# Eight feed-forward tile pairs done jointly instead of six, fewer dense matmuls between attention's steps, and two groups of vector work with a higher priority

## The chip, the cores and the metric

The kernel runs on one core of one Trainium2 chip. The metric is the device time of one execution in microseconds; lower is better. Of three timed runs the median is 1756.36 us (1756.19 to 1757.58).

## The reference

One layer of a hybrid decoder, 1024 tokens wide and long (D = S = 1024), in float32:

```
u = rmsnorm(x);  proj = u @ w_in
y_a = rwkv7_mix(token_shift(p_rwkv), ...)          # 8 heads of 64
y_b = dsa_attention(q, k, v, q_idx, k_idx, w_idx)  # 8 heads of 64, causal, top 256 keys by an indexer
merged = sigmoid(g_a) * (y_a @ w_o_rwkv) + sigmoid(g_b) * (y_b @ w_o_att)
h = x + merged @ w_out
z_gate, z_up = split(rmsnorm(h) @ w_ffn_in)        # 1024 -> 2 x 2816
h = h + (silu(z_gate) * z_up) @ w_ffn_out          # 2816 -> 1024
return rmsnorm(h)
```

## The kernel before

The tokens are cut in two halves of HT = 512. Activations lie transposed, 8 planes of 128 channels by 512 tokens. Every large matrix product is done in three matmuls for each 128-row plane of the contraction: high part of the weights by high part of the activations (L143), high by low (L144), low by high (L148). `split` makes such a pair: ACT copies x to `hi` (L117), DVE subtracts it to give `lo` (L118). Weights come by DMA on SP's queue into `wst` (ring of 3) and are split into `whi` and `wlo` (rings of 2). Results gather in PSUM: 3 banks `acc`, 5 banks `mix`.

The feed-forward part has 22 tiles of 128 columns (gate and up each) in three groups: `GROUPS = [(0, 8), (8, 8), (16, 6)]`. For the first two groups each half does `ffn_in` (the two products, then silu times up) and `ffn_out` (a partial product with `w_ffn_out`, 128 output channels at a time, added to the residual that lies in DRAM as `d_h`: load, add at L1388, store). The third group (`JOINT = 2`) is done for both halves at once by `joint`: as in Winograd's form of Strassen's scheme, the four block products of a tile pair become 7 products of 12 matmuls each, 84 where two halves apart take 96. For it DVE and ACT make sums and differences of the activations of both halves: T1 (from L1604), T2 (L1592, L1610) and the split of B22 ahead of the joint loop, T3 (L1592) and T4 (L1633, L1634) inside its first round. `h` is normalised there by L1575 with `row` (L287 spreads it on PE, L294 copies it). The old activations of half 0 are read back from `d_z`. m1 and m2 are the products with half 0's own planes `za` and `zb`; m1 and m2 of the first two pairs stand ahead of the loop, those of pair j + 2 in round j: T1, m1, T2, B22, T3, m2, T4. The result of each round goes to DRAM (`d_f`), and `reload` brings it back as an `ffn_out` operand, `fhi`/`flo` for half 0 and `fj` for half 1.

What sets the order. PE's order is the order of the program text (`manual_schedule`). A queue `fill` holds generators of dense matmuls, and `pump(n)` issues about n of them between the steps of something else. The attention of half 1 (`attend`, 4 head pairs of 4 query blocks, 16 units) yields after each step how many to pump: logits (L1100, then on DVE bias and minimum L1102, on ACT the exponential L1105), transposes (L1114, copied by ACT at L1116), values (L1124). While it runs, the fill is ffn_in and ffn_out of half 0. The order of the other engines is made by a list scheduler; `tc.high_priority()` moves what stands under it ahead. Each engine does its own list in that order, and waits where an operand isn't there.

At the end: attention of half 1, `merge` (w_o, w_out, the residual h of half 1), then `joint`, in whose front the rest of the fill, ffn_out of half 0, group 1, is issued (`run(*fill)`) between L287 and m1; then dense tiles of half 1 with ffn_out and norm of half 0 between them, ffn_out of half 1, and `finish_out`: the last group's partial product for half 1, the last residual add and the norm, transposed for the last 128 tokens.

In `normalise` (half 0, in the first group, while RWKV runs) `zb`, planes 4 to 7 of the normalised activations, is split last.

Of the kernel before, what the change touches and what calls it, by code (L numbers as in the profile page):

```python
# [12 lines left out]
F32R = mybir.dt.float32r  # L13
# [6 lines left out]
ALU = mybir.AluOpType  # L20
# [3 lines left out]
S = 1024  # L24
HT = 512
NFF = 22
GROUPS = [(0, 8), (8, 8), (16, 6)]
JOINT = 2
TOPK = 256
C1 = math.exp(-0.5)  # L30
# [20 lines left out]
def block_kernel(ctx: ExitStack, tc: tile.TileContext, ins: dict, outT: bass.AP, outR: bass.AP, stop=None, dbg=None):  # L51
# [64 lines left out]
    def split(hi, lo, x):  # L116
        A.activation(hi, x, AF.Copy)  # L117
        V.tensor_tensor(lo, x, hi.bitcast(F32), op=ALU.subtract)  # L118
# [8 lines left out]
    def weights(src, nk=8, rush=True, st=None, pool=None):  # L127
        with tc.high_priority() if rush else nullcontext():
            if st is None:
                st = raw_weights(src, nk)  # L130
            hi, lo = ((pool or wp).tile([128, nk, 128], F32R, tag=tag, name=tag, bufs=8 if pool else None)
                      for tag in ("whi", "wlo"))
            split(hi, lo, st)
        return hi, lo
# [115 lines left out]
    def opened(side, name, **kw):  # L250
        stack = ExitStack()
        return stack, stack.enter_context(tc.tile_pool(name=name, bufs=1, side=side, reuse_waits="tile", **kw))
# [810 lines left out]
    def attend(half, p, bias):  # L1063
# [112 lines left out]
        for i in range(len(units) + 2):  # L1176
            if i < len(units):
                hp, bi = units[i]
                if i == 0:
                    kqv[hp] = load(hp)  # L1180
                    load_q(hp, 0)
                    load_q(hp, 1)
                if bi == 2 and hp < 3:
                    kqv[hp + 1] = load(hp + 1, sms[hp][:, 0, :] if half else None)
                    load_q(hp + 1, 0)
                    load_q(hp + 1, 1)
                if bi == 0:
                    sms[hp] = smp.tile([128, 4, 2], F32, tag="sm", name="sm", bufs=3)
                Ls[i] = []
            for e in range(2):  # L1190
                if i < len(units):
                    Ls[i].append(logits(hp, bi, e, kqv[hp], sms[hp]))
                    yield 4 if half else (bi + 3) // 2
                if 0 <= i - 1 < len(units):
                    ptss.setdefault(i - 1, []).append(turn(units[i - 1][1], Ls[i - 1][e]))
                    yield 3 if half else (units[i - 1][1] + 3) // 2
            if i >= 2:
                hp2, bi2 = units[i - 2]
                if bi2 == 0:
                    pys[hp2] = mix()  # L1200
                values(bi2, ptss.pop(i - 2), kqv[hp2], pys[hp2])
                if bi2 == 3:
                    ri = close1(sms[hp2])
                yield 3 if half else bi2 + 1
                if bi2 == 3:
                    closing.append((2, hp2, ri))
                elif closing:
                    close(closing)
# [85 lines left out]
    def normalise(zp, sq, row):  # L1294

        h = sq.h

        def one(k, out):
            V.scalar_tensor_tensor(out, h[:, k, :], par[:, P_N2 + k:P_N2 + k + 1], row, op0=ALU.mult, op1=ALU.mult)
            SY.dma_start(d_z[k], out)  # L1300

        low, ts = zp.tile([128, 8, HT], F32R, tag="s2", name="za"), []
        for k in range(4):
            one(k, h[:, k, :])
            split(low[:, k, :], low[:, 4 + k, :], h[:, k, :])
        for k in range(4):
            ts.append(tmp() if k < 3 else tp.tile([128, HT], F32, tag="sacc", name="zt", bufs=2))
            one(4 + k, ts[k])
        high = zp.tile([128, 8, HT], F32R, tag="s0", name="zb")
        for k in range(4):  # L1310
            split(high[:, k, :], high[:, 4 + k, :], ts[k])
        return [Planes(*(a + b)) for a, b in zip(parts(low), parts(high))]

    def ffn_in(zp, tags, zs, gi, box):
# [47 lines left out]
    def ffn_out(half, zp, f, gi, sqs=None):  # L1362
        gn = GROUPS[gi][1]
        final = sqs is not None
        if final:
            h = zp.tile([128, 8, HT], F32, tag="s2", name="h")
            sqs.append(Rms(h))
            for d in range(8):
                G.dma_start(h[:, d, :], d_h[half][d])

        def w(d):
            return weights(ins["w_fo1"][d] if final else ins["w_fo0"][gi, d], gn)

        bank = mix if final else acc
        pss = [bank() for _ in range(1 if final else 2)]
        last = yield from but_last(mm3_last(pss, [w(d) for d in range(len(pss))], f, gn, within=half == 1))
        for d in range(8):
            if final:
                t = h[:, d, :]
            else:  # L1380
                t = tmp()
                SY.dma_start(t, d_h[half][d])
            if d < len(pss):
                ps = pss[d]
            else:
                ps = bank()
                last = yield from but_last(mm3(ps, w(d), f, nk=gn))
            V.tensor_tensor(t, t, ps, op=ALU.add)  # L1388
            if final:
                sqs[0].add(d)  # L1390
            else:
                SY.dma_start(d_h[half][d], t)
            if d >= len(pss) - 1:
                yield last
# [25 lines left out]
    def finish_out(half, zp, f):  # L1420

        gn, n = GROUPS[-1][1], HT - 128
        tok, last = slice(0, n), slice(n, HT)
        h = zp.tile([128, 8, HT], F32, tag="s1", name="h")
        for d in range(8):
# [63 lines left out]
            V.tensor_scalar(out[:, 512:768], hT[:, 512:768], rs, None, op0=ALU.mult)  # L1491
            SY.dma_start(outR[:, 512:1024], out[:, 512:1024])

    def ffn(half, zp, zs, tags):

        for gi in range(JOINT):
            f = []
            yield from ffn_in(zp, tags, zs, gi, f)
            yield from ffn_out(half, zp, f[0], gi)

    def joint(z0, zp0, zs1, zp1, md, after):

# [262 lines left out]
    sz0, zp0 = zps[0]  # L1765
    sr.close()
    with tc.tile_pool(name="at1", bufs=1, side="right", reuse_waits="tile") as ap:
        pump(130)
        for n in attend(1, ap, bias):
            pump(abs(n))  # L1770
    sb.close()
    (sz1, zp1), zs1, sq0 = opened("right", "zp1"), [], []
    smd, md = opened("right", "md")
    stage_j = joint(z0[0], zp0, zs1, zp1, md,
                    lambda z1: fill.append(ffn(1, zp1, [z1, None], ("s3", "s0"))))
    run_over(merge(1, zp1, zs1, next(stage_j)))
    next(stage_j)
    smd.close()
    fj = act_tiles(zp0, "f", ("s1", "s0"))
    reload(0, fj)  # L1780
    credit[0] = 0
    pump_whole(144 - 8)
    run_over(ffn_out(0, zp0, fj, JOINT, sq0))
    pump_whole(48)
    run_over(norm_out(0, sq0[0]))
    pump(300)
    sz0.close()
    sfj, fp = opened("right", "fj")
    fj = tuple(fp.tile([128, GROUPS[JOINT][1], HT], F32R, name=f"fj{i}") for i in range(2))
    reload(1, fj)  # L1790
    run(*fill)
    finish_out(1, zp1, fj)
    sfj.close()
    sz1.close()


# [20 lines left out]
def _layout(x, norm1_g, w_in, tshift_mu, w_decay_up, w0, a_up, a0, g_up, k_k, k_a, r_k,  # L1817
# [8 lines left out]
    a = {}  # L1826
# [26 lines left out]
    wi = cols(w_ffn_in)  # L1853
    a["w_ffn_in"] = np.ascontiguousarray(np.stack([wi[:NFF], wi[NFF:]], axis=1).reshape(2 * NFF, 128, 8, 128))
    wo = cols(w_ffn_out)
    a["w_fo0"] = np.ascontiguousarray(np.stack([wo[:, :, 0:8], wo[:, :, 8:16]], axis=0))
    a["w_fo1"] = np.ascontiguousarray(wo[:, :, 16:22])
    return a


# [15 lines left out]
```

## Time and the profile before

| | |
|---|---|
| median of 3 runs | 1756.36 us |
| the profiled execution | 1753.59 us, span 1751.7 us |
| mean granted clock of TensorE | 0.988 |
| PE busy | 97% |
| DVE, ACT, POOL busy | 64%, 50%, 8% |
| DMA | 253 MB, 145 GB/s over the span |

The page's times are those of one execution. A group's line names the source line, the engine, the operation, out<-in, the shape and the count, then the busy time and what ended the idle time before it. PE's busy time is modelled and overlaps between neighbouring matmuls, so the cost of a matmul is read from the distance between starts, not from its own length.

### The profile page before, as it was taken

What the parts mean: (1) busy time and instruction counts of PE and PEld (TensorE: products, weight loads), DVE (VectorE), ACT (ScalarE), POOL (GpSimd) and SP (SyncE); (2) the same over time, 40 slices, a digit from 0 to 9 for tenths busy, and PEclk for the clock granted to TensorE, in tenths of its full rate; (3) what the DMA queues carried; (4) which work ended last, traced back from release to release, by engine and by line L of the source; (5) the groups of instructions that cost most, each with busy time, mean ns of one, the idle gap of its engine ahead of it and who ended that gap; (6) DMA issues with size and microseconds to landing.
All of it is one profiled execution on the core that took longest, in us unless ns stands there. A gap on an engine that the chain in (4) does not pass through costs nothing.

```text
span 1751.7 us, 26667 instructions
## 1 busy us (share of the span) xinstructions
PE 1694.3 (97%) x10000; PEld 1395.7 (80%) x10000; DVE 1127.6 (64%) x2206; ACT 869.6 (50%) x1685; POOL 133.8 (8%) x183
## 2 busy tenths in 40 slices
PE   8999999999999999999999999999979999999997
PEld 6888888888878777877787888888857788888887
DVE  6789899866577567858856544466577655433344
ACT  6365998554455788665334365533334333222322
POOL 0000000010022110001000311011000100000001
PEclk9999999999999999999999999999989999999999
DMA  5542334545376436734343764266622633553362
GB/s 209 178 139 87 107 91 141 174 108 160 109 214 169 146 102 197 225 112 137 90 121 100 228 172 127 91 226 203 187 83 90 193 112 108 172 168 102 115 214 80
DMA packets 144448, 253.44 MB, mean 145 GB/s; under 512 B 49680, under 2 KB 71888, under 8 KB 144192
## 3 DMA queue, kind: packets, MB, share of 16 engines
q1 hardware_dynamic: 115760, 161.84, 29.8%
q10 hardware_dynamic: 16128, 48.60, 8.8%
q0 software_dynamic: 12432, 41.30, 8.1%
q8 instruction: 79, 1.29, 0.3%
q14 instruction: 49, 0.40, 0.1%
HBM read 193.45 MB, written 58.25 MB: 144 GB/s over the span
## 4 chain that ended last, share of the span: by engine, by line
PE 41%; issue 6%; DVE 2%; DMA 1%; ACT 1%; POOL 1%; POOLq 0%; DVEq 0%; ACTq 0%
PE acc L148 9%; PE acc L143 9%; PE acc L144 9%; PE acc L161 3%; PE mix L1124 1%; PE mix L1100 1%; PE mix L1114 1%; PE mix L1548 1%; PE mix L1546 1%; PE mix L1545 1%; PE mix L148 1%; PE mix L144 1%; PE mix L143 1%; DMA wst<-in_w_ffn_in 0%; DMA d_h<-tmp 0%
## 5 line engine op out<-in xcount | busy, mean ns | idle before, releaser
L118 DVE TENSOR_TENSOR wlo<-wst,whi 128x1024 fp32r<-128x1024 f32 (+1 forms) x203 | 248.1, 1223 | 246.0 <-ACT whi L117 130.0
L117 ACT ACTIVATE whi<-wst 128x1024 fp32r<-128x1024 f32 (+1 forms) x203 | 212.6, 1049 | 278.4 <-PE acc L144 212.5
L143 PE MATMUL acc<-u1hi,whi 128*128 128x512 f32 x320 | 127.9, 400 | 0.0
L144 PE MATMUL acc<-u1lo,whi 128*128 128x512 f32 x320 | 125.1, 391 | 0.0
L143 PE MATMUL acc<-u0hi,whi 128*128 128x512 f32 (+1 forms) x320 | 122.8, 386 | 0.0
L144 PE MATMUL acc<-u0lo,whi 128*128 128x512 f32 (+1 forms) x320 | 121.3, 382 | 0.0
L143 PE MATMUL acc<-s,whi 128*128 128x512 f32 x256 | 99.8, 390 | 0.0
L144 PE MATMUL acc<-s,whi 128*128 128x512 f32 x256 | 99.6, 389 | 0.0
L143 PE MATMUL acc<-fhi,whi 128*128 128x512 f32 x192 | 76.9, 401 | 12.6 <-DVE tmp L1388 12.6
L148 PE MATMUL acc<-u1hi,wlo 128*128 128x512 f32 x320 | 81.8, 394 | 0.0
L148 PE MATMUL acc<-u0hi,wlo 128*128 128x512 f32 (+1 forms) x320 | 78.6, 384 | 0.0
L144 PE MATMUL acc<-flo,whi 128*128 128x512 f32 x192 | 76.0, 396 | 0.0
L1015 ACT ACTIVATE junkl<-kept,z 128x1024 int8<-128x1024 int16 (+1 forms) x64 | 69.4, 1084 | 4.7 <-DVE kept L984 4.4
L143 PEld LDWEIGHTS acc<-u1hi,whi 128*128 128x128 f32 x320 | 60.1, 188 | 12.6 <-issue 0.9
L1105 ACT ACTIVATE L<-L,mx 128x128 f32<-128x128 f32 (+7 forms) x64 | 49.5, 774 | 41.4 <-DVE mx L1102 40.8
L143 PEld LDWEIGHTS acc<-u0hi,whi 128*128 128x128 f32 x320 | 60.2, 188 | 11.9 <-issue 0.4
L144 PEld LDWEIGHTS acc<-u1lo,whi 128*128 128x128 f32 x320 | 60.2, 188 | 11.3
L144 PEld LDWEIGHTS acc<-u0lo,whi 128*128 128x128 f32 x320 | 60.2, 188 | 11.0
L148 PEld LDWEIGHTS acc<-u1hi,wlo 128*128 128x128 f32 x320 | 58.9, 188 | 12.5 <-issue 0.9
L148 PEld LDWEIGHTS acc<-u0hi,wlo 128*128 128x128 f32 x320 | 58.1, 188 | 11.9 <-issue 0.7
L148 PE MATMUL acc<-s,wlo 128*128 128x512 f32 x256 | 63.2, 389 | 0.0
L148 PEld LDWEIGHTS acc<-s,wlo 128*128 128x128 f32 x256 | 48.0, 188 | 10.0
(476 smaller groups left out, 4080.7 us busy)
## 6 DMA issues: line engine op xcount, KB each, us to landing
wst<-in_w_ffn_in SPq DMA_DIRECT2D x61, 512.0 KB
wst<-in_w_in ACTq DMA_DIRECT2D x36, 512.0 KB
wst<-in_w_in SPq DMA_DIRECT2D x27, 512.0 KB
wst<-in_w_fo SPq DMA_DIRECT2D x25, 512.0 KB
k<-d_k POOLq DMA_DIRECT2D x24, 512.0 KB, 8.0
d_g<-tmp ACTq DMA_DIRECT2D x32, 256.0 KB
wst<-in_w_ffn_in ACTq DMA_DIRECT2D x16, 512.0 KB
tmp<-d_h SPq DMA_DIRECT2D x32, 256.0 KB
```

The lines of the kernel that those rows point to most:

```text
L117: A.activation(hi, x, AF.Copy)
L118: V.tensor_tensor(lo, x, hi.bitcast(F32), op=ALU.subtract)
L143: T.matmul(ps, whi[:, wk + k, :], ahi[:, ak + k, tok], start=k == 0, stop=False)
L144: T.matmul(ps, whi[:, wk + k, :], alo[:, ak + k, tok], start=False, stop=False)
L148: T.matmul(ps, wlo[:, wk + k, :], ahi[:, ak + k, tok], start=False, stop=k == nk - 1)
L161: T.matmul(ps, w[:, k, :], a[:, k, tok], start=k == 0 and j == 0, stop=k == nk - 1 and j == 2)
L1015: A.activation(junka[:, :n], y, AF.Sign, bias=z[:, i:i + 1], accum_out=cnt[:, i:i + 1])
L1100: T.matmul(ps[:, :w], q[bi // 2][:, e, bi % 2 * 128:bi % 2 * 128 + 128], k[:, i, e, c:c + w], start=i == 0, stop=i == 1)
L1105: A.activation(L[:, :n], L[:, :n], AF.Exp, scale=-1.0, bias=last, accum_out=sm[:, bi, e:e + 1])
L1114: T.transpose(ps[:, j * 128:(j + 1) * 128], L[:, (c + j) * 128:(c + j + 1) * 128], ident)
L1124: T.matmul(py[64 * e:64 * e + 64, bi * 128:(bi + 1) * 128], v[:, j, 64 * e:64 * e + 64], pts[e][j // 4][:, j % 4, :], start=j == b, stop=j ...
L1545: T.matmul(ps, whi[:, k, :], hi[k], start=opens and k == 0, stop=False, skip_group_check=True)
```

## The change

- `GROUPS` becomes `[(0, 8), (8, 6), (14, 8)]`: 8 pairs are done jointly, and the second group has 6 tiles. The host's layout of `w_ffn_out` follows (`w_fo0` holds the two groups of 8, `w_fo1` that of 6).
- In half 1, attention pumps 3, 2 and 2 after logits, transposes and values, where it pumped 4, 3 and 3; ahead of it `pump(100)` instead of `pump(130)`.
- In `normalise` the splits of zb have high priority (the late split).
- In `ffn_out`, where it isn't the final one, the residual add has high priority.
- For half 1 the joint group is reloaded right after half 0's, and its ffn_out comes after the first dense group; the group of 6 stays in SBUF and is what `finish_out` multiplies last.

```diff
-GROUPS = [(0, 8), (8, 8), (16, 6)]
+GROUPS = [(0, 8), (8, 6), (14, 8)]
...
-                    yield 4 if half else (bi + 3) // 2
+                    yield 3 if half else (bi + 3) // 2
...
-                    yield 3 if half else (units[i - 1][1] + 3) // 2
+                    yield 2 if half else (units[i - 1][1] + 3) // 2
...
-                yield 3 if half else bi2 + 1
+                yield 2 if half else bi2 + 1
...
-        for k in range(4):
-            split(high[:, k, :], high[:, 4 + k, :], ts[k])
+        with tc.high_priority():
+            for k in range(4):
+                split(high[:, k, :], high[:, 4 + k, :], ts[k])
...
-            return weights(ins["w_fo1"][d] if final else ins["w_fo0"][gi, d], gn)
+            return weights(ins["w_fo1"][d] if gi == 1 else ins["w_fo0"][gi // 2, d], gn)
...
-            V.tensor_tensor(t, t, ps, op=ALU.add)
+            with nullcontext() if final else tc.high_priority():
+                V.tensor_tensor(t, t, ps, op=ALU.add)
...
-        gn, n = GROUPS[-1][1], HT - 128
+        gn, n = GROUPS[1][1], HT - 128
...
-    def ffn(half, zp, zs, tags):
+    def ffn(half, zp, zs, tags, fj=None, kept=None):
...
-            yield from ffn_out(half, zp, f[0], gi)
+            if gi == 0 or kept is None:
+                yield from ffn_out(half, zp, f[0], gi)
+            else:
+                kept.append(f[0])
+            if gi == 0 and fj is not None:
+                yield from ffn_out(half, zp, fj, JOINT)
...
-        pump(130)
+        pump(100)
...
+    fj1, f1 = [], []
     stage_j = joint(z0[0], zp0, zs1, zp1, md,
-                    lambda z1: fill.append(ffn(1, zp1, [z1, None], ("s3", "s0"))))
+                    lambda z1: fill.append(ffn(1, zp1, [z1, None], ("s3", "s0"), fj1, f1)))
...
     reload(0, fj)
+    sfj, fp = opened("right", "fj")
+    fj1.extend(fp.tile([128, GROUPS[JOINT][1], HT], F32R, name=f"fj{i}") for i in range(2))
+    reload(1, fj1)
...
-    pump(300)
+    run(*fill)
+    fill.clear()
+    sfj.close()
     sz0.close()
-    sfj, fp = opened("right", "fj")
-    fj = tuple(fp.tile([128, GROUPS[JOINT][1], HT], F32R, name=f"fj{i}") for i in range(2))
-    reload(1, fj)
-    run(*fill)
-    finish_out(1, zp1, fj)
-    sfj.close()
+    finish_out(1, zp1, f1[0])
```

The lines above L1388 keep their numbers or move by one; those below move by 2 to 8 (the residual add L1388 is L1390 after, L1575 is L1582, L1604 is L1611, L1592 is L1599, L1610 is L1617, L1645 is L1652, L1554 is L1561).

How the order moves, at three places. First PE in attention, at the fourth block of a head pair (512 wide logits), before:

```order
L1124 MATMUL mix<-pt,v 64x128 x10
L1100 MATMUL mix<-k,q 128x512 x4
L143 MATMUL acc<-zb,whi 128x512
L144 MATMUL acc<-zb,whi 128x512
L143 MATMUL acc<-zb,whi 128x512
L144 MATMUL acc<-zb,whi 128x512
L1114 MATMUL mix<-kc,L 128x128 x7
L148 MATMUL acc<-za,wlo 128x512 x4
L1100 MATMUL mix<-k,q 128x512 x4
L148 MATMUL acc<-zb,wlo 128x512 x4
L1114 MATMUL mix<-kc,L 128x128 x7
L1124 MATMUL mix<-pt,v 64x128 x12
```

and with the change:

```order
L148 MATMUL acc<-za,wlo 128x512 x4
L1124 MATMUL mix<-pt,v 64x128 x10
L1100 MATMUL mix<-k,q 128x512 x4
L148 MATMUL acc<-zb,wlo 128x512 x4
L1114 MATMUL mix<-kc,L 128x128 x7
L1100 MATMUL mix<-k,q 128x512 x4
L1114 MATMUL mix<-kc,L 128x128 x7
L143 MATMUL acc<-za,whi 128x512
L144 MATMUL acc<-za,whi 128x512
L143 MATMUL acc<-za,whi 128x512
L144 MATMUL acc<-za,whi 128x512
L1124 MATMUL mix<-pt,v 64x128 x12
```

The dense matmuls (L143, L144, L148) between the first transposes and the second logits, and between those and the second transposes, are gone. Over the whole attention of half 1 the dense matmuls between steps go from 272 to 195, and the pairs of steps with none between them from 16 to 35.

Second, DVE in the joint front. Before, from the last of T2's and B22's splits (the `s` tiles here) on, with the residual adds L1388 behind:

```order
L118 TENSOR_TENSOR s_12329<-h,s_12329 128x512
L1592 TENSOR_TENSOR t_12324<-h 128x512
L118 TENSOR_TENSOR s_12296<-t_12314,s_12296 128x512
L1610 TENSOR_TENSOR t_12322<-t_12322,t_12324 128x512
L118 TENSOR_TENSOR s_12329<-h,s_12329 128x512
L1388 TENSOR_TENSOR tmp<-tmp,acc 128x512
L118 TENSOR_TENSOR s_12296<-t_12322,s_12296 128x512
L1388 TENSOR_TENSOR tmp<-tmp,acc 128x512 x2
```

and with the change, from the start of the normalisation on (here `s` is T1):

```order
L1582 SCALAR_TENSOR_TENSOR h<-h,par,row 128x512 x2
L1611 TENSOR_TENSOR t_12119<-h,t_12119 128x512
L1611 TENSOR_TENSOR t_12125<-h,t_12125 128x512
L1582 SCALAR_TENSOR_TENSOR h<-h,par,row 128x512
L1390 TENSOR_TENSOR tmp<-tmp,acc 128x512
L118 TENSOR_TENSOR wlo<-wst,whi 128x768
L118 TENSOR_TENSOR s_12117<-t_12119,s_12117 128x512
L118 TENSOR_TENSOR s_12117<-t_12125,s_12117 128x512
L1611 TENSOR_TENSOR t_12131<-h,t_12131 128x512
L1582 SCALAR_TENSOR_TENSOR h<-h,par,row 128x512
L1390 TENSOR_TENSOR tmp<-tmp,acc 128x512
```

The residual adds stand among T1's operations now, each ahead of the splits of T1 that follow it; one more comes behind the last rows shown. ffn_out of half 0 has 56 matmuls left behind L287 where it had 88.

Third, ACT at the second joint pair, before (`whi` is for m1 of the fourth pair, `sw` are sums of weights):

```order
L117 ACTIVATE sw<-sr 128x512
L117 ACTIVATE sw<-wst 128x512
L1665 ACTIVATE tmp<-u_12630 128x512
L117 ACTIVATE s_12571<-tmp 128x512
L117 ACTIVATE whi<-wst 128x1024
```

and with the change (L1652 copies the round's first product, m5):

```order
L117 ACTIVATE sw<-sr 128x512
L117 ACTIVATE sw<-wst 128x512
L1652 ACTIVATE tmp<-acc 128x512
L117 ACTIVATE whi<-wst 128x1024
L117 ACTIVATE sw<-sr 128x512
L1561 ACTIVATE tmp<-mix 128x512
```

Here the copy stands ahead of `whi`; at the zb splits, which the priority of `normalise` is about, ACT's and DVE's rows are the same before and after.

More of the change, by code (lines that the diff above doesn't have):

```diff
@@ L1855, in _layout @@
     wo = cols(w_ffn_out)
-    a["w_fo0"] = np.ascontiguousarray(np.stack([wo[:, :, 0:8], wo[:, :, 8:16]], axis=0))
-    a["w_fo1"] = np.ascontiguousarray(wo[:, :, 16:22])
+    a["w_fo0"] = np.ascontiguousarray(np.stack([wo[:, :, 0:8], wo[:, :, 14:22]], axis=0))
+    a["w_fo1"] = np.ascontiguousarray(wo[:, :, 8:14])
     return a
```

## The prediction

> **What bounds the kernel now.** I read the engine totals first, then the list of what PE waits for, then the three places in that list which the change touches, in the timeline.
>
> ```profile
> span 1751.7 us, 26667 instructions
> PE 1694.3 (97%) x10000; PEld 1395.7 (80%) x10000; DVE 1127.6 (64%) x2206; ACT 869.6 (50%) x1685; POOL 133.8 (8%) x183
> ```
>
> PE is busy 97% of the span, so the kernel ends when PE has gone through its list. A change pays in two ways only: fewer matmuls, or fewer waits between them. The price of one matmul comes from two stretches without a wait (columns: stretch, length, busy time and count of PE, PEld, DVE, ACT, POOL, granted clock, DMA share, GB/s); three stretches used below stand with the first.
>
> ```profile
> 1550.00:1600.00 50.00, 50.00 (x222) 41.42 (x221) 17.79 (x20) 12.01 (x13) 0.00 (x0) 1.00 0.49 142
> ...
> 998.90:1137.00 138.10, 137.44 (x1022) 114.95 (x1022) 66.21 (x164) 80.24 (x157) 19.82 (x37) 1.00 0.46 126
> 1256.50:1283.40 26.90, 14.33 (x63) 11.61 (x62) 23.99 (x37) 9.88 (x15) 2.79 (x5) 0.85 0.45 145
> 1283.40:1321.10 37.70, 35.93 (x151) 28.78 (x150) 26.15 (x42) 14.33 (x23) 2.19 (x4) 0.97 0.21 70
> ```
>
> 50 us hold 222 matmuls of 128x512: 0.225 us each, at full clock. The waits of PE, longest first (us in total, times, longest):
>
> ```profile
> PE acc L143 <- DVE tmp L1388: 12.6, 1, 12.6
> PE acc L427 <- ACT u0hi L300: 6.9, 1, 6.9
> PE mix L622 <- DVE x L698: 3.4, 1, 3.4
> PE acc L143 <- ACT zb L117: 3.3, 1, 3.3
> ...
> PE mix L1545 <- DVE tmp L1670: 1.7, 1, 1.7
> ...
> PE mix L1545 <- ACT s L117: 1.2, 1, 1.2
> ...
> PE mix L1546 <- DVE s L118: 0.6, 2, 0.3
> PE mix L1100 <- ACT pt L1116: 0.5, 2, 0.3
> ```
>
> The longest one stands in front of the joint tiles. PE needs a free bank of `acc`, which the residual add of L1388 frees, and that add stands on DVE behind the splits of T1, T2 and B22. The timeline of PE and DVE there (start, length, engine, line; in brackets the idle time before and its releaser):
>
> ```profile
> 1254.81 1.05 PE L287 MATMUL mix<-kc,rs 128*128 128x128 f32 x8
> 1282.97 0.77 PE L143 MATMUL acc<-fhi,whi 128*128 128x512 f32 x1 [12.57 <-DVE tmp L1388]
> 1283.54 0.63 PE L144 MATMUL acc<-flo,whi 128*128 128x512 f32 x1
> 1285.67 0.44 PE L143 MATMUL acc<-fhi,whi 128*128 128x512 f32 x1
> 1321.46 0.86 PE L1548 MATMUL mix<-s,sw 128*128 128x512 f32 x3
> ...
> 1256.53 1.41 DVE L1575 SCALAR_TENSOR_TENSOR h<-h,par,row 128x512 f32<-128x512 f32 x2 [1.47 <-ACT row L294]
> 1281.55 0.68 DVE L118 TENSOR_TENSOR s<-h,s 128x512 fp32r<-128x512 f32 x1
> 1282.15 0.68 DVE L1388 TENSOR_TENSOR tmp<-tmp,acc 128x512 f32<-128x512 f32 x1
> 1282.75 0.68 DVE L118 TENSOR_TENSOR s<-t,s 128x512 fp32r<-128x512 f32 x1
> 1259.72 1.22 DVE L118 TENSOR_TENSOR wlo<-wst,whi 128x1024 fp32r<-128x1024 f32 x1
> 1260.86 1.28 DVE L118 TENSOR_TENSOR s<-t,s 128x512 fp32r<-128x512 f32 x2
> 1266.36 0.69 DVE L1604 TENSOR_TENSOR t<-h,t 128x512 f32<-128x512 f32 x1 [1.69 <-DMA t<-d_z]
> 1278.53 0.69 DVE L1610 TENSOR_TENSOR t<-t,t 128x512 f32<-128x512 f32 x1 [1.20 <-DMA t<-d_z]
> ```
>
> DVE works through 23.99 us in 26.90 while PE stands; successive 128x512 operations start 0.60 us apart (1281.55, 1282.15, 1282.75) and a 1024-wide split takes 1.14 (1259.72 to 1260.86). After the wait the matmuls run at half clock: from 1283.54 to 1285.67 five of them start 0.43 us apart. That costs some 1.4 us more with the slow first one (0.57).
>
> **The sum, part by part.** Time zero for the joint front is the start of L287 (1254.81); the matmul count between any two points is from the order of both kernels.
>
> *Eight pairs, not six.* A joint pair has 7 products of 12 matmuls, 84, where two separate tiles have 96. Two pairs more are 24 matmuls less, and the order of PE holds just that: 24 x 0.225 = **-5.4 us**. The additional transforms of weights fall on DVE, ACT and SP, in the joint loop; its cover there is PE's own 84 matmuls (18.9 us) per pair against some 11 us of DVE work, worked out as about 18 operations of 0.60. If the cover failed, each pair would wait on L1670 or the weight splits, as the 1.7 us did once before.
>
> *Residual adds in front.* Before, T4's last matmuls start at 1321.46 and end 0.7 later, at t = 67.3. Between L287 and the joint products PE has 88 matmuls of ffn_out before and 56 now, 32 less (7.2 us, which moved elsewhere and are no gain), so like for like the old front ends at 60.1. Now DVE starts on the normalisation at t = 1.7. It has the same splits, but each add of a finished ffn_out tile stands between T1's operations and frees its bank as PE ends the tile (every 18 x 0.225 = 4.1 us); the 12.6 us wait has no cause left. In exchange DVE's T1 splits queue behind those adds, each waiting for PE. From there to T2's last split the new order has 35 operations of 128x512 (three of them adds), a 768-wide and two 1024-wide weight splits: 35 x 0.60 + 0.86 + 2 x 1.14 = 24.1 us, so t = 25.8 if nothing waits; with the two waits for d_z of before, 1.69 and 1.20, it is 28.7, and I take 29. Unhindered, PE would reach T2 after 0.8 us of L287 and 128 matmuls, at 29.6, and T4's end after 188, at 43.1; so DVE is late next, at T4 above all. From T2's last split to T4's last split the order has 32 operations of 0.60 and a split of 1.14, 20.3 us; T4 then ends one us later (its four last matmuls), at 29 + 20.3 + 1.0 = 50.3. Gain: 60.1 - 50.3 = 9.8. Against it I set 1.3 us at the second pair, whose `whi` split now stands on ACT behind the copy of m5 (bounds 0 and the 2.7 us of one product of 12), and 0.5 for the clock. Together **-8.0 us**. Bounds: the same way took 37.70 us before, in step with PE, which was busy 35.93 of them; DVE's own part was 26.15 (row 1283.40, 42 operations). If the new one needs all 26.15, the gain is 60.1 - 56.2 = 3.9; if nothing waits, 60.1 - 43.1 = 17.0. I take the count of operations, since residual adds and weight splits that swelled the old row stand earlier now.
>
> The clock, by rows: a wait of 1.75 us was followed by matmuls at full clock, one of 3.34 by half clock.
>
> ```profile
> 821.93 0.80 PE L143 MATMUL acc<-zb,whi 128*128 128x512 f32 x1 [3.34 <-ACT zb L117]
> 824.10 0.63 PE L143 MATMUL acc<-zb,whi 128*128 128x512 f32 x1
> 1392.85 0.50 PE L1545 MATMUL mix<-s,sw 128*128 128x512 f32 x1 [1.75 <-DVE tmp L1670]
> 1393.19 0.40 PE L1546 MATMUL mix<-s,sw 128*128 128x512 f32 x1
> 821.01 0.21 ACT L117 ACTIVATE nr<-nr 128x16 fp32r<-128x16 f32 x1 [3.56 <-POOL nr L652]
> 821.25 0.63 ACT L117 ACTIVATE zb<-tmp 128x512 fp32r<-128x512 f32 x1
> ```
>
> The new wait for T4 comes in pieces (m1 of the third pair, then T4's third and fourth plane), the largest some 3.5 us. It lies between those rows' ends, nearest to 3.34, so a 1.4 us loss is a matter of luck: 0.5. [...]
>
> *Late split.* The zb splits on ACT stand behind `nr`, which waits 3.56 us for POOL (rows 821.01 and 821.25). The new priority would have to put them ahead; in the new order ACT and DVE have the same rows there, so I cost it at **0**, and the 3.3 us wait stays. [...]
>
> *Fewer dense matmuls between attention's steps.* Attention of half 1 runs with almost no wait now:
>
> ```profile
> 1004.31 0.62 PE L1100 MATMUL mix<-k,q 128*128 128x384 f32 x2 [0.23 <-ACT pt L1116]
> 1096.87 0.86 PE L1100 MATMUL mix<-k,q 128*128 128x320 f32 x4 [0.31 <-ACT pt L1116]
> ...
> L1105 ACT ACTIVATE L<-L,mx 128x640 f32<-128x640 f32 (+3 forms) x32 | 31.6, 987 | 21.4 <-DVE mx L1102 21.1
> ```
>
> In its order 272 dense matmuls stand between the steps now and 195 after, so it shrinks by 77 x 0.225 = 17.3 us from 138.1, and those matmuls run elsewhere: no gain. ACT has 80.24 us of work there and DVE 66.21, so no engine but PE is full. What can go wrong is a step whose predecessor's result isn't ready. Steps that follow each other without a dense matmul between rise from 16 to 35. The 16 cost 0.54 us in all, 0.03 each; the two that waited cost 0.23 and 0.31. So 35 cost between 1.2 and 10.9 us. I take 4.0, 0.11 each: nearer the low end, because most of the 35 are values-then-logits and transpose-then-logits, where only a `mix` bank is wanted; but at the fourth block of each head pair transposes follow logits bare, and there an exponential (987 ns mean) and L1102 lie between. Less the 0.5 of today: **+3.5 us**.
>
> *Tail.* ffn(1) now ends with ffn_in of six tiles, and finish_out reads them from SBUF. The last f tile, the first h loads and the first free bank come then directly before finish_out's matmuls. The `wf` splits have run ahead; f's last plane is used last. Bounds 0 and 2 (no wait there today), I take **+0.3**. Reloading eight tiles instead of six puts two more loads and splits for each half ahead of the next dense weights:
>
> ```profile
> 1423.56 2.29 ACT L117 ACTIVATE fj<-fj 128x512 fp32r<-128x512 f32 x4 [0.84 <-DMA fj<-d_f]
> ...
> 1426.27 1.04 ACT L117 ACTIVATE whi<-wst 128x1024 fp32r<-128x1024 f32 x1
> 1434.98 0.85 ACT L117 ACTIVATE whi<-wst 128x768 fp32r<-128x768 f32 x1 [1.13 <-PE acc L144]
> ```
>
> The split at 1434.98 waited for PE to end 16 matmuls (3.6 us) with the weights of 1426.27, so PE began those at 1431.3, 4.0 us after they were ready. Two more copies at 0.57 us fit; **+0.5** for contention of the loads with weights. If that cover is gone, the four copies cost 2.3.
>
> Sum: -5.4 - 8.0 + 0 + 3.5 + 0.3 + 0.5 = **-9.1 us**. The profiled execution took 1753.59 (span 1751.7), so its like would take 1744.5. That execution stands 2.8 under the median of 1756.36; against the median I predict **1747.3**.
>
> **Rivals.** (a) *DVE keeps ahead in the front*: the residual adds never wait, T2 and T4 are ready in time. For it: DVE has 14 us less to wait for. Against it: by the counts above DVE ends T4's splits at 25.8 + 20.3 = 46.1 even if it never waits, and PE would end T4 at 43.1. Then at best -5.4 - 17.0 + 4.3 = -18.1, 1738.3. Chance 0.13. (b) *The wait only moves*: the adds wait for PE, T1 behind them, and DVE needs its old 26 us from T2 to T4. For it: row 1283.40. Then -5.4 - 3.9 + 1.8 + 4.3 = -3.2, 1753.2, hardly to be told from no change. Chance 0.19. (c) *Slower: attention becomes bound by its own chain* of logits, exponential, transpose and copy. Place: the 35 bare steps; price: if each waits 0.6 us, about an exponential less the transposes of one head, 21 us; then -5.4 - 8.0 + 20.5 + 0.8 = +7.9, 1764.3. It decides above (13.4 - 0.8 + 0.5 + 3.5) / 35 = 0.47 us each. Against it: the dearest bare wait now is 0.31. Chance 0.08. (d) *The front's priority does nothing*, as that of the late split: the order shows the adds moved, so I give it no chance of its own. The forecast itself has 0.60, with a range of its own of 1742 to 1752.
>
> The range for all: from (a), 1738.3, to just above (b), 1756. Below lie 0.07, above 0.12. A change of 0.2% is 3.5 us, about the least that can be told from none. Faster by more (below 1752.9) holds the forecast, (a) and a part of (b): 0.77. Slower by more is (c) with a little of a failed tail: 0.08. The rest, 0.15, is the same.
>
> **What will show it.** In the waits of PE: no `acc` wait on the residual add above 1 us; new waits on `wlo`, `tmp` or `s` splits in the joint front of 5 to 10 us together; waits of L1100 and L1114 summing to 2 to 7 us in attention; the 3.3 us of zb unchanged. In a stretch without waits the pitch stays at 0.225. I am wrong if the front's waits stay above 14 us or vanish, or if attention's pass 10.

## The result and the profile after

The change takes 1748.06 us (median of 5 runs, 1742.49 to 1749.80) against 1756.19 before (5 runs, 1755.12 to 1757.58): a ratio of 0.9945 (of the means), 95% interval 0.9926 to 0.9964. That is 8.1 us less by the medians and 9.7 by the means; 1747.3 was forecast. The profiled execution took 1748.32 us, span 1746.5.

The page's totals and the waits of PE, longest first:

```profile
span 1746.5 us, 26655 instructions
PE 1691.7 (97%) x9976; PEld 1391.6 (80%) x9976; DVE 1135.9 (65%) x2224; ACT 872.5 (50%) x1695; POOL 136.5 (8%) x187
```

```profile
PE acc L427 <- ACT u0hi L300: 6.6, 1, 6.6
PE mix L622 <- DVE x L698: 3.4, 1, 3.4
PE acc L143 <- ACT zb L117: 3.3, 1, 3.3
...
PE mix L1552 <- ACT whi L117: 2.8, 1, 2.8
PE mix L1552 <- ACT sw L117: 2.5, 1, 2.5
...
PE mix L1114 <- ACT pt L1116: 2.1, 4, 0.6
...
PE mix L1552 <- DVE tmp L1677: 1.7, 1, 1.7
...
PE mix L1552 <- ACT u L1666: 1.6, 1, 1.6
PE mix L1555 <- DVE wlo L118: 1.4, 1, 1.4
```

PE has 24 matmuls less (10000 to 9976). The 12.6 us wait on the residual add has left the list. What stands in its place is spread over the joint front, as the timeline of PE shows; L1552, L1553 and L1555 are the old L1545, L1546 and L1548, the three terms of a product (the DVE row is explained below):

```profile
1234.12 1.05 PE L287 MATMUL mix<-kc,rs 128*128 128x128 f32 x8
1264.68 1.20 PE L1555 MATMUL mix<-za,wlo 128*128 128x512 f32 x4 [1.36 <-DVE wlo L118]
1279.28 0.76 PE L1552 MATMUL mix<-s,sw 128*128 128x512 f32 x1 [2.51 <-ACT sw L117]
1278.45 0.68 DVE L1677 TENSOR_TENSOR tmp<-mix,tmp 128x512 f32<-128x512 f32 x1
1282.60 0.50 PE L1552 MATMUL mix<-s,sw 128*128 128x512 f32 x1 [0.43 <-ACT s L117]
1283.74 0.50 PE L1553 MATMUL mix<-s,sw 128*128 128x512 f32 x1 [0.65 <-DVE s L118]
1285.01 0.40 PE L1552 MATMUL acc<-s,sw 128*128 128x512 f32 x1
1290.71 0.50 PE L1552 MATMUL mix<-za,whi 128*128 128x512 f32 x1 [2.81 <-ACT whi L117]
```

L287 starts at 1234.12, T4 of the first pair is through at 1285.01: 50.9 us. The first four waits come to 4.95 us, the one at the second pair to 2.81. The row of 2.51 us names an ACT copy of `sw` that this product doesn't read. By the program it adds to the bank that L1677 must read first; L1677 ended on DVE at 1279.13, 0.06 us before that copy, behind the splits of T4's first two planes. So this wait, too, is one for DVE. Attention waits in four places, once in each head pair, and each time at its fourth block:

```profile
1013.40 0.98 PE L1114 MATMUL mix<-kc,L 128*128 128x128 f32 x7 [0.45 <-ACT pt L1116]
1044.54 0.55 PE L1114 MATMUL mix<-kc,L 128*128 128x128 f32 x3 [0.56 <-ACT pt L1116]
1075.23 0.55 PE L1114 MATMUL mix<-kc,L 128*128 128x128 f32 x3 [0.56 <-ACT pt L1116]
1105.91 0.55 PE L1114 MATMUL mix<-kc,L 128*128 128x128 f32 x3 [0.56 <-ACT pt L1116]
```

One trap lies in setting the two spans side by side: they differ by 5.2 us only. Up to the 6200th matmul, shortly ahead of attention, PE has the same instructions in the same order in both kernels (on DVE the residual adds move at the end of that stretch, from 924 us on); there the execution of the change took 966.2 us from the first matmul on, that of before 963.0. From there to the last matmul it is 762.2 against 770.9, 8.7 less. I call this second stretch the *rest*, and use it below beside the ratios, because the first stretch differs from run to run even where the order is the same on every engine (last section).

### The profile page after: what moved, and what is told of

Read it like the earlier page. It is cut to its first block, busy times and chain, and to the rows that moved or that the text cites. A ratio compares the mean times of both kernels' runs of the same rounds, so it can differ in the third digit from the quotient of the medians.

```text
span 1746.5 us, 26655 instructions
## 1 busy us (share of the span) xinstructions
PE 1691.7 (97%) x9976; PEld 1391.6 (80%) x9976; DVE 1135.9 (65%) x2224; ACT 872.5 (50%) x1695; POOL 136.5 (8%) x187
## 4 chain that ended last, share of the span: by engine, by line
PE 42%; issue 6%; DVE 2%; ACT 1%; DMA 1%; POOL 1%; POOLq 0%; DVEq 0%; ACTq 0%
PE acc L143 8%; PE acc L144 8%; PE acc L148 8%; PE acc L161 3%; PE mix L1124 1%; PE mix L1552 1%; PE mix L1555 1%; PE mix L1553 1%; PE mix L1100 1%; PE mix L1114 1%; DMA wst<-in_w_ffn_in 1%; PE mix L143 1%; PE mix L148 1%; PE mix L144 1%; PE acc L1555 1%
## 5 line engine op out<-in xcount | busy, mean ns | idle before, releaser
L118 DVE TENSOR_TENSOR wlo<-wst,whi 128x1024 fp32r<-128x1024 f32 (+1 forms) x197 | 240.1, 1220 | 186.3 <-ACT whi L117 94.3
L117 ACT ACTIVATE whi<-wst 128x1024 fp32r<-128x1024 f32 (+1 forms) x197 | 206.3, 1049 | 271.1 <-PE acc L144 200.1
L143 PE MATMUL acc<-u1hi,whi 128*128 128x512 f32 x320 | 128.4, 401 | 0.0
L144 PE MATMUL acc<-u1lo,whi 128*128 128x512 f32 x320 | 125.5, 392 | 0.0
L143 PE MATMUL acc<-u0hi,whi 128*128 128x512 f32 (+1 forms) x320 | 122.8, 387 | 0.0
L144 PE MATMUL acc<-u0lo,whi 128*128 128x512 f32 (+1 forms) x320 | 121.3, 382 | 0.0
L143 PE MATMUL acc<-s,whi 128*128 128x512 f32 x224 | 87.3, 390 | 0.0
L144 PE MATMUL acc<-s,whi 128*128 128x512 f32 x224 | 87.2, 389 | 0.0
L148 PE MATMUL acc<-u1hi,wlo 128*128 128x512 f32 x320 | 81.8, 395 | 0.0
L148 PE MATMUL acc<-u0hi,wlo 128*128 128x512 f32 (+1 forms) x320 | 78.6, 384 | 0.0
L143 PEld LDWEIGHTS acc<-u1hi,whi 128*128 128x128 f32 x320 | 60.3, 188 | 12.6 <-issue 0.9
L143 PEld LDWEIGHTS acc<-u0hi,whi 128*128 128x128 f32 x320 | 60.1, 188 | 11.9 <-issue 0.4
L144 PEld LDWEIGHTS acc<-u1lo,whi 128*128 128x128 f32 x320 | 60.4, 189 | 11.4
L144 PEld LDWEIGHTS acc<-u0lo,whi 128*128 128x128 f32 x320 | 60.2, 188 | 11.0
L148 PEld LDWEIGHTS acc<-u1hi,wlo 128*128 128x128 f32 x320 | 58.9, 188 | 12.6 <-issue 0.9
L148 PEld LDWEIGHTS acc<-u0hi,wlo 128*128 128x128 f32 x320 | 58.1, 188 | 11.9 <-issue 0.7
L1390 DVE TENSOR_TENSOR tmp<-tmp,acc 128x512 f32<-128x512 f32 x32 | 21.8, 684 | 62.2 <-PE acc L148 48.5
L148 PE MATMUL acc<-s,wlo 128*128 128x512 f32 x224 | 55.3, 389 | 0.0
L143 PE MATMUL acc<-fhi,whi 128*128 128x512 f32 x132 | 53.5, 406 | 0.0
L1015 ACT ACTIVATE junk<-sc,z 128x640 bf16<-128x640 int16 (+1 forms) x64 | 49.0, 765 | 8.1 <-DVE z L1019 7.8
```

The lines of the kernel that those rows point to most:

```text
L143: T.matmul(ps, whi[:, wk + k, :], ahi[:, ak + k, tok], start=k == 0, stop=False)
L144: T.matmul(ps, whi[:, wk + k, :], alo[:, ak + k, tok], start=False, stop=False)
L148: T.matmul(ps, wlo[:, wk + k, :], ahi[:, ak + k, tok], start=False, stop=k == nk - 1)
L1015: A.activation(junka[:, :n], y, AF.Sign, bias=z[:, i:i + 1], accum_out=cnt[:, i:i + 1])
```

## The experiments

Two theories. Theory 1: in the joint front DVE's chain from `row` to T4's last split, some 50 us, sets the end; the dense matmuls of ffn_out behind L287 are cover, and the adds' priority only pays because it lets PE use this cover. Theory 2: PE's own list sets the front as soon as no add is late; each pair pays its 2.7 us, and where the dense matmuls stand makes no difference. The rival of the prediction that ends slower, attention bound by its own chain, is tested beside them. Every ratio is to runs of the kernel before on the same chip. (1) to (11) number the runs of the table at the end of this section.

**(1) Old yields.** The edit, on the changed kernel:

```diff
-        pump(100)
+        pump(130)
...
-                    yield 3 if half else (bi + 3) // 2
+                    yield 4 if half else (bi + 3) // 2
-                    yield 2 if half else (units[i - 1][1] + 3) // 2
+                    yield 3 if half else (units[i - 1][1] + 3) // 2
-                yield 2 if half else bi2 + 1
+                yield 3 if half else bi2 + 1
```

> The changed kernel with attention's old yields (4, 3, 3) and 130 ahead of it. In the order no ffn_out matmul is left behind L287, where the change has 56. Theory 1 (from row to T4's last split DVE sets the end of the joint front, and dense matmuls up to there are free cover): T4 ends about 45 us behind L287 against 50.9 with the change, though PE has 12.6 us less to do there; waits in the front of 14 to 18 us; attention's waits back at 0.5; about 1754 us, 6 above the change. Theory 2 (PE's own list sets the front once the residual adds are gone, and where the dense matmuls stand is all one): 1746 to 1748, and attention's 1.6 us gained.

Measured: ratio 1.0030 (1.0017 to 1.0042), slower than before. Waits of PE in the stretch 1225 to 1312:

```profile
PE mix L1555 <- DVE wlo L118: 8.1, 1, 8.1
PE mix L274 <- DVE sacc L268: 4.5, 1, 4.5
PE mix L1552 <- ACT s L117: 2.1, 1, 2.1
PE mix L287 <- POOL rs L280: 1.4, 1, 1.4
```

The 16 us of waits are as forecast, but two of them, 5.8 us, stand a step earlier than I had looked: the chain of the norm (the last square, its sum, the power on POOL) is bare, without dense matmuls beside it, as well. I had put the time at 1754; the median is 1760.37. Part of the 6 us lies outside the front: the last matmul of the fill is issued at 1150.9, and behind it `merge` waits 3.5 us for DVE's splits of `ylo` and `mlo` (1153 to 1205), where the change has no such wait. Half clock is likely to account for more, though its share isn't measured: the record of the granted clock shows 23.9 us at half speed in this front and 3.4 in `merge`, against 3.4 in both together with the change (mean over the execution 0.983 against 0.989). So the smaller yields are not there for attention's sake. They hold back the matmuls that the front needs. Theory 2 falls.

**(2) Without the adds' priority.**

```diff
-            with nullcontext() if final else tc.high_priority():
-                V.tensor_tensor(t, t, ps, op=ALU.add)
+            V.tensor_tensor(t, t, ps, op=ALU.add)
```

> The changed kernel without the high priority of the residual adds. Theory 1: four adds stand behind B22 again, PE waits for an acc bank from the third tile on, 12 to 17 us and at half clock after it; T4 is ready when PE comes; 1755 to 1758 us. Theory 2 (the wait went because the group of 6 has shorter tiles and fewer of them, not because of the priority): no acc wait above 2 us, about 1748.

Measured: 1.0002 (0.9991 to 1.0014), the time of before. The long wait is back, in front of an ffn_out tile:

```profile
1256.13 0.77 PE L143 MATMUL acc<-fhi,whi 128*128 128x512 f32 x1 [15.28 <-ACT s L117]
...
1255.31 1.28 DVE L1389 TENSOR_TENSOR tmp<-tmp,acc 128x512 f32<-128x512 f32 x2
```

The row names ACT's last split, since the wait is put down to what came last; by the order it is the bank that the add frees. The first add (L1389 here) starts at 1255.31, 0.60 us before the second, so it was done some 0.1 us before PE went on; it stands on DVE behind all but one of the splits of T2 and B22. The whole gain of the change hangs on this priority.

**(3) The adds' priority alone**, on the kernel before: the same two lines the other way round, nothing else.

> The kernel before with the high priority of the residual adds and nothing else: six pairs, old yields, 88 matmuls in the front. Theory 1: the 12.6 us wait goes, 88 matmuls cover DVE's way to T4 almost wholly (PE would reach T4's end 50.3 us behind L287, DVE some 50), waits in the front under 4 us; 1741 to 1745 us, below the change. Rival: the wait only moves from the adds to T2 and T4, 1752 to 1756.

Measured: 0.9915 (0.9897 to 0.9934), 1741.01 us: below the change, with six pairs and the old yields. (The two intervals still overlap, from 0.9926 to 0.9934; that of (5), with six pairs too, lies clear of the change.) All that PE waits for in the stretch 1225 to 1312:

```profile
PE mix L1546 <- ACT s L117: 1.2, 1, 1.2
PE mix L1547 <- DVE s L118: 0.8, 2, 0.5
```

88 matmuls cover DVE's chain but for 2.0 us. This one line gives 13.8 us in the rest, and with everything else of the change it comes to 8.7.

**(4) Less ahead of attention**, to put a tile more into the front: `pump(60)` for `pump(100)`.

> The changed kernel with 60 matmuls ahead of attention, not 100. In the order one more ffn_out tile, 18 matmuls, stands behind L287: 74. Theory 1: 4.1 us more cover, so the front's waits fall from 7.8 us to about 4 and the clock may stay up; 1742 to 1745 us, if attention's first loads are there after 40 matmuls (9 us) less. Theory 2: 1748, or more by a wait of L1100 for its first keys.

Measured: 0.9966 (0.9953 to 0.9980): not better than the change. Two reasons, one for each end:

```profile
988.37 1.41 PE L1100 MATMUL mix<-k,q 128*128 128x320 f32 x4 [8.34 <-DMA q<-d_q]
...
1285.67 0.77 PE L1552 MATMUL mix<-s,sw 128*128 128x512 f32 x1 [6.48 <-DVE tmp L1677]
```

Attention's first queries aren't there: the 40 matmuls, 9 us, had covered their load. And in the front the waits stay at 7.2 us in spite of 74 matmuls. T4 adds to the bank that L1677 must read first, and in this order L1677 stands on DVE behind T4's last split; in the change it stands ahead of the last two. My forecast of 4 us took DVE's order for unchanged, and it isn't: each change of the text reorders it.

**(5) The adds' priority and the new yields, six pairs**: the fourth corner of pairs by yields.

> Six pairs, with the priority of the residual adds and with the new yields (3, 2, 2, and 100 ahead): the fourth corner of pairs by yields. 157 ffn_out matmuls stand behind L287. Theory 1 (the front needs some 88 matmuls of cover for DVE's chain, more bring nothing): front waits as with the adds alone, 2 us; attention's 2.1 us of waits; 1742 to 1744, one or two above the adds alone. Rival (more cover is better still, or the bare steps cost more than their waits show): below 1739, or above 1747.

Measured: 0.9902 (0.9883 to 0.9920). The waits are those forecast, 2.3 us in the front and 2.1 in attention; the rest takes 757.3 us, with the adds alone 757.1. So the yields by themselves cost nothing that can be measured, and a cover of 157 matmuls brings nothing over 88.

**(6) T4's subtractions on POOL**: `G.tensor_tensor` for the two `V.tensor_tensor` of each plane of T4.

> The changed kernel with the eight subtractions that make T4 (L1640, L1641) on POOL instead of DVE. If DVE's chain sets the end of the front: T4's last split comes up to 8 x 0.60 = 4.8 us sooner, front waits fall from 7.8 us by 3 to 5; 1743 to 1746. If PE's place in the order or the weight splits set it: 1748, no change; slower, if POOL (some 1.3 us for each, from 1.01 us for 384 columns) becomes the last one: T4 later, 1750 or more.

Measured: 0.9959 (0.9945 to 0.9973), no faster than the change; the rest takes 765.6. POOL became the last one, on its own queue:

```profile
1273.81 1.36 POOL L1640 TENSOR_TENSOR tmp<-tmp,s 128x512 f32<-128x512 f32 x1 [0.88 <-DMA tmp<-d_z]
...
1280.78 1.59 POOL L1641 TENSOR_TENSOR tmp<-tmp,s 128x512 f32<-128x512 f32 x1
1282.32 0.56 POOL L1591 DMA_DIRECT2D tmp<-d_z  x1
1285.28 1.41 POOL L1640 TENSOR_TENSOR tmp<-tmp,s 128x512 f32<-128x512 f32 x1 [2.40 <-DMA tmp<-d_z]
```

POOL also issues the loads of d_z. The fourth is now issued behind six subtractions of 1.3 to 1.6 us and lands 3 us later, and PE waits 4.46 us for that plane. DVE loses time as well: beside POOL's subtractions three of its 128x512 operations (1281.17, 1285.48, 1287.16) take 1.75 us each, where 0.69 is usual in this front. So this run doesn't show what a shorter DVE chain is worth; it shows that T4's last plane is what the front ends on, whichever engine makes it.

**(7) Seven pairs**: `GROUPS = [(0, 8), (8, 7), (15, 7)]` in the changed kernel, the layout of the weights to match.

> The changed kernel with groups of 8, 7 and 7: seven pairs, new yields, 100 ahead, adds' priority. 87 ffn_out matmuls stand in the front, as many as in the kernel before (88). Theory 1: with this cover the front's waits are about those of the adds alone, 2 to 4 us, attention's 2.1; 12 matmuls less than with six pairs, 2.7 us; 1740 to 1742, below the change by 6 to 8 though it has a pair less. Theory 2 (each pair pays 2.7 us and the front is all one): 1750 to 1751, 2.7 above the change.

Measured: 0.9882 (0.9863 to 0.9902), 1738.18 us: clearly below the change with a pair less. Its waits in the front:

```profile
1288.05 0.47 PE L1552 MATMUL mix<-s,sw 128*128 128x512 f32 x1 [2.09 <-DVE tmp L1677]
...
1290.36 0.50 PE L1553 MATMUL mix<-s,sw 128*128 128x512 f32 x1 [0.45 <-DVE s L118]
```

Again as theory 1 has it: 87 matmuls in the front, 2.5 us of waits.

**(8) Yields of 2, 1 and 1** in the changed kernel.

> The changed kernel with attention's yields cut again, to 2, 1 and 1. 74 ffn_out matmuls in the front. Theory: attention's waits rise well above 2.1 us, since most steps stand bare; if each of some 50 bare steps waits 0.5 us, as the four did, 25 us, the front gains 2 to 4, and the time is 1760 to 1770. If the steps hide behind each other as most do now: attention 4 to 6 us, about 1747.

Measured: 0.9944 (0.9927 to 0.9961), the time of the change. Attention's waits:

```profile
PE mix L1114 <- ACT pt L1116: 0.9, 1, 0.9
PE mix L1114 <- ACT L L1105: 0.6, 1, 0.6
PE mix L1100 <- DVE mx L1102: 0.3, 1, 0.3
PE mix L1100 <- ACT pt L1116: 0.3, 1, 0.3
```

2.1 us again, in other places. The first branch, 0.5 us for each bare step, is out, and the 4 to 6 us of the second were too many as well. The front has 74 matmuls and waits 8.0 us, 6.7 of them for L1677 as in (4).

**(9) Without the late split's priority.**

> The changed kernel without the priority of the zb splits. Every engine has the same instructions in the same order as in the change, so by the order the late split does nothing: the same time, 1748 us within the spread of single runs (about 1742 to 1750), the same 3.3 us wait of PE for zb. If the priority does something that the order does not show: above 1751.

Measured: 0.9950 (0.9930 to 0.9970), with the same wait for zb, 3.34 us. The late split as written does nothing: in the trace the order of PE, DVE and ACT is that of the change throughout. So this run also is a second execution of the change, and shows how far the rest agrees with itself: 760.9 against 762.2.

**(10) A late split that works**: the high part of zb on DVE.

```diff
-                split(high[:, k, :], high[:, 4 + k, :], ts[k])
+                V.tensor_copy(high[:, k, :], ts[k])
+                V.tensor_tensor(high[:, 4 + k, :], ts[k], high[:, k, :].bitcast(F32), op=ALU.subtract)
```

> The changed kernel with the high parts of zb copied on DVE instead of ACT, so that they no longer queue behind nr, which waits for POOL. DVE is idle there for 3.7 us. If ACT's queue is what PE waits for: the 3.3 us wait of PE shrinks to under 1 us, and with the half clock behind it 3 to 6 us are gained, 1742 to 1745 us. If not (the normalisation itself is late): the wait stays, 1748.

Measured: 0.9925 (0.9898 to 0.9952), which overlaps with the change (0.9926 to 0.9964): not settled. PE's timeline there says why little is left:

```profile
822.12 0.50 PE L144 MATMUL acc<-zb,whi 128*128 128x512 f32 x1 [0.44 <-DVE zb L1313]
...
832.45 0.77 PE L143 MATMUL acc<-za,whi 128*128 128x512 f32 x1 [5.49 <-DVE tmp L1339]
```

The 3.3 us wait is down to 0.9 (two of 0.44), and PE, 4.7 us ahead of its place in the change, runs into the next one: 5.49 us for a bank that L1339 frees. That operation comes no sooner: counted from the last za matmul ahead of zb it starts on DVE after 10.8 us, and in the change (L1338) after 10.4.

**(11) Yields of 1, 1 and 1**, eight pairs with a full cover of 114 matmuls.

> The changed kernel, eight pairs, with attention's yields 1, 1 and 1. 114 ffn_out matmuls stand in the front. Theory 1 (pairs pay 2.7 us each once the front has some 88 matmuls of cover): front waits about 2 us, attention's waits 2 to 6; a ratio to the kernel before of 0.986 to 0.989, at or below that of seven pairs (0.9882). Rival: attention is bound at last, since most of its steps are bare; its waits pass 10 us and the ratio is 0.992 or more.

Measured: 0.9901 (0.9873 to 0.9929). All of attention's waits and all of the front's:

```profile
PE mix L1114 <- DVE mx L1102: 0.6, 2, 0.3
PE mix L1114 <- ACT pt L1116: 0.5, 1, 0.5
```

```profile
PE mix L1552 <- ACT s L117: 1.2, 1, 1.2
PE mix L1553 <- DVE s L118: 0.5, 2, 0.3
PE acc L143 <- ACT whi L117: 0.3, 1, 0.3
```

Attention isn't bound even now; its 1.1 us are below the 2 to 6 that I expected. With the front covered, the eight pairs come to the level of (5) and (7), and against the change this saves 7.3 us in the rest. The ratio is a little above what I expected, and the intervals of (3), (5), (7) and (11) overlap, so the ratios don't rank six, seven and eight pairs. By the rest, (11) is the shortest: 754.9 us, against 756.4 with seven pairs and 757.1 to 757.3 with six. Two pairs more, 5.4 us of matmuls, thus leave 2.3 us, and with 1.3 us between two executions of one order (9) even that ranking is open. Part of the difference is new waits of 3.3 us at the end of the joint loop (1.62 and 1.70), where six pairs have 1.7; the remainder I have not traced.

| kernel | pairs | yields | adds first | matmuls in the front | waits in the front, us | rest, us | ratio (95%) |
|---|---|---|---|---|---|---|---|
| before | 6 | 4 3 3 | no | 88 | 14.4 | 770.9 | 1 |
| the change | 8 | 3 2 2 | yes | 56 | 7.8 | 762.2 | 0.9945 (0.9926 to 0.9964) |
| (1) | 8 | 4 3 3 | yes | 0 | 16.2 | 778.2 | 1.0030 (1.0017 to 1.0042) |
| (2) | 8 | 3 2 2 | no | 56 | 16.8 | 770.8 | 1.0002 (0.9991 to 1.0014) |
| (3) | 6 | 4 3 3 | yes | 88 | 2.0 | 757.1 | 0.9915 (0.9897 to 0.9934) |
| (4) | 8 | 3 2 2, 60 ahead | yes | 74 | 7.2 | 769.0 | 0.9966 (0.9953 to 0.9980) |
| (5) | 6 | 3 2 2 | yes | 157 | 2.3 | 757.3 | 0.9902 (0.9883 to 0.9920) |
| (6) T4 on POOL | 8 | 3 2 2 | yes | 56 | 10.0 | 765.6 | 0.9959 (0.9945 to 0.9973) |
| (7) | 7 | 3 2 2 | yes | 87 | 2.5 | 756.4 | 0.9882 (0.9863 to 0.9902) |
| (8) | 8 | 2 1 1 | yes | 74 | 8.0 | 763.3 | 0.9944 (0.9927 to 0.9961) |
| (9) no late split | 8 | 3 2 2 | yes | 56 | 8.2 | 760.9 | 0.9950 (0.9930 to 0.9970) |
| (10) zb on DVE | 8 | 3 2 2 | yes | 56 | 7.8 | 761.6 | 0.9925 (0.9898 to 0.9952) |
| (11) | 8 | 1 1 1 | yes | 114 | 2.0 | 754.9 | 0.9901 (0.9873 to 0.9929) |

"Waits in the front" are those of PE from L274 to m1 of the fourth pair; the columns from the matmuls to the rest are of one profiled execution each. In (5) and (11) 0.5 and 0.3 us of them are a wait for `whi` at an ffn_out tile.

The traces also show directly how long DVE's chain is. Behind the start of L287, T4's last split ends on DVE after 46.0 us with no cover (1), 49.6 with 56 matmuls (the change), 52.3 with 88 (3), 58.5 with 114 (11) and 68.5 with 157 (5). DVE idles in it for 6.3, 4.3, 2.5, 5.4 and 14.4 us. So from 0 to 88 matmuls, 19.8 us of PE's time, the chain grows by 6.3 us only, since the cover isn't free for DVE: each ffn_out tile brings it an add and a weight split (no add in (1), 4 in the change and in (3), 8 in (11) and (5)). With 157 matmuls DVE has no more to do than with 114 and idles 9 us longer: there it no longer sets the end.

## Why the prediction was right, step by step

- *24 matmuls less, -5.4.* The page counts 24 less. In the stretch 1550 to 1600, without a wait, 50 us hold 222 matmuls as before.
- *The residual adds in front, -8.0.* T4 was to be through 50.3 us behind L287, and was at 50.9. The way there was close as well: T2's last split ended at 28.2 (29 taken), T4's at 49.6 (49.3). At T2 two errors cancel: the waits for d_z were 0.2 us, not 2.9, but an add and a weight split of 1.5 us together stood on DVE ahead of the normalisation. Like for like that is 60.1 - 50.9 = 9.2 gained. At the second pair PE lost 2.81 us where I took 1.3: there I had bounds of 0 and 2.7 and chose the middle, and the upper one was passed. The copy of m5 is only a part of it:

```profile
1284.80 0.69 DVE L1545 TENSOR_TENSOR sr<-wst 128x512 f32<-128x512 f32 x1
1288.00 0.60 ACT L1652 ACTIVATE tmp<-acc 128x512 f32<-128x512 f32 x1 [1.25 <-PE acc L1555]
1289.60 1.06 ACT L117 ACTIVATE whi<-wst 128x1024 fp32r<-128x1024 f32 x1 [1.00 <-DMA wst<-in_w_ffn_in]
```

The copy ended at 1288.60, and the split waited 1.00 us more, for the load of its weights. SP issued that load at 1285.55, as soon as L1545 on DVE had read the old weights out of the ring. I had no term for it. In (10), where the split follows the copy without a wait, PE waits 1.69 us. So the term is -6.4 instead of -8.0. The half clock is contained in the 50.9. The term's mechanism, DVE becoming the last one at T4, is shown by (1) and (11), where only the yields and what is pumped ahead of attention change (0 and 114 matmuls of cover, 16.2 and 2.0 us of waits), and agrees with (3) and (7), where pairs or yields differ too. (4) and (8) show its limit: a tile more of cover gains nothing when L1677 falls behind T4's last split.

- *The late split, 0.* Shown by (9).
- *Attention, +3.5.* Measured 2.1 - 0.5 = 1.6. The places were right (the fourth block, where logits and transposes of the second head stand bare), the size was half. 31 of the 35 bare steps wait for nothing.
- *Tail and reload, +0.3 and +0.5.* No wait in the tail. The dense weights behind the reload were not late either; but the end of the joint loop waits 3.31 us (1.57 and 1.74) where it waited 2.0, so +1.3, at a place that I had not costed. The pair turns up in (8) and (11) too, but in (9), with the order of the change, only the second wait is there (1.73). So the +1.3 is of this execution and isn't a settled cost.

Sum of the measured terms: -5.4 - 6.4 + 1.6 + 1.3 = -8.9, against 8.7 in the rest, 8.1 in the medians and 9.7 in the means. That the forecast of 1747.3 is within 1 us of the median is partly luck: the front gained 1.6 less than forecast and attention cost 1.9 less, which nearly cancels. The rivals: (a), nothing left to wait for, is what (3) and (7) do, and needs more cover than the change leaves; (b), the wait only moves, came true for about a half of the 14.4 us, though not for its reason: DVE needed 21.4 us from T2 to T4, not its old 26; (c), attention bound by itself, fell with (8) and (11).

What I had not seen is that the change gives away a part of what it gains. The two pairs more take dense tiles out of half 0's own fill; the smaller yields give some of that back to the front, and 56 matmuls are left of 88. That is why one line of the change, alone, is worth 13.8 us in the rest, and the whole 8.7.

On the clock: I had placed the point at which a wait halves it between 1.75 and 3.34 us. (The 3.5 us that I expected lay beyond 3.34, not between.) The runs show no such point. With the change, a wait of 2.51 us is followed by half clock (starts 0.43 us apart):

```profile
1279.28 0.76 PE L1552 MATMUL mix<-s,sw 128*128 128x512 f32 x1 [2.51 <-ACT sw L117]
1279.84 0.63 PE L1553 MATMUL mix<-s,sw 128*128 128x512 f32 x1
```

By the granted clock half speed lasts here from 1279.01 to 1282.42. In (10) full clock goes on for 1.2 us behind a wait of 2.98 us (starts 0.23 us apart from 1276.89 to 1277.81). The matmul of 1277.81, ahead of the next wait, already takes 0.59 us instead of 0.39, and from 1283.18 to 1284.46 the starts lie 0.43 us apart:

```profile
1276.58 0.47 PE L1553 MATMUL mix<-s,sw 128*128 128x512 f32 x1 [2.98 <-ACT sw L117]
1276.89 0.39 PE L1554 MATMUL mix<-s,sw 128*128 128x512 f32 x1
...
1277.81 0.59 PE L1554 MATMUL mix<-s,sw 128*128 128x512 f32 x1
1279.74 0.80 PE L1553 MATMUL mix<-s,sw 128*128 128x512 f32 x1 [1.34 <-ACT s L117]
```

In (7) a wait of 2.09 us is followed by full clock (starts 0.23 us apart), and in (11) three waits of 0.19, 1.18 and 0.32 us within 3 us by half clock (0.43 us apart from 1276.90 on). So in these runs the length of a single wait doesn't decide it.

What the granted clock of two records shows besides: in the change the half-speed stretches ahead of the last one are 3.4 or 6.8 us long and start at 586.11, 678.26, 749.94, 825.04, 848.93, 930.85 and 1279.01; in the kernel before they are 3.4, 6.8 or 10.2 us long and start at 674.78, 821.56, 845.45, 937.61 and 1275.53. Within each record the distances between these starts are, to 0.1 us, multiples of the shortest stretch, 3.413 us (from 825.04 to 848.93 it is 7 times that). What makes the clock fall at one of these places and not at another isn't shown.

## What to carry to other kernels

When an engine other than the bound one has a long chain between two stages, independent work of the bound engine placed beside that chain is worth its length there until it covers the chain (here 16.2 us of waits with no matmul beside it, 2.0 with 88, 2.3 with 157), and little elsewhere: count it as a stock, and ask of each change what it takes out of the stock. Work that frees a buffer for the bound engine goes ahead of long preparations on its engine: here one add of 0.6 us, behind the splits of T1, T2 and B22, held PE for 12.6 us. And test the parts of a bundled change alone: here one line, alone, came out ahead of the whole (13.8 us in the rest against 8.7).

## What the runs showed of the hardware

The same instructions take different times from run to run. Ten of the profiled executions (all but those of the kernel before, (2) and (10)) have the same order on every engine up to shortly ahead of the 6200th matmul. The way there from the first matmul took from 961.3 us (7) to 966.9 us (6), 0.6%. The granted clock falls at other places from run to run (up to 924 us the kernel before has the same order too: the change runs at half clock for 3.4 us from 586.11 and from 749.94, and before at full clock there), but the sum of the half-speed stretches on that way does not order the runs: behind the first one, at the start, it is 23.9 us both in (7) and in (6). Nor is it the start: by the 100th matmul (6) is 0.5 us behind (7). The rest comes in steps, at places where PE waits for ACT or DVE in one execution and not in the other (at 433.29 in (6) by 0.81 us, in (7) not at all); why those engines are late there stays open. For a change of half a per cent two spans mislead by more than a third of the effect (here 5.2 us instead of 8.1). The stretch behind the point where the kernels part is better, but not exact: between the change and (9), which have the same order, it differs by 1.3 us.
